# Dealing the columns of gathered expert rows over the U and V blocks: 42, 26, 35 and 33 instead of 45, 26, 35 and 30

## The chip, the cores and the metric

The kernel runs on one core of a Trainium2 chip. The metric is the device time of one execution in microseconds, as the median of several executions; less is better. "The profiled execution" is one more execution, recorded by the hardware profiler.

## The reference

One inference step of a hybrid decoder: a trunk layer (a Conformer convolution module and a Mamba-2 mixer that share their projections) and behind it a PEER expert mixer, which takes more than half of the time and which alone the change touches. It reads, cut to what matters:

```python
def peer_block(xb, w_q, keys, U, V):
    T = xb.shape[0]
    q = (xb @ w_q).reshape(T, PEER_HEADS, 2, D_KEY // 2)
    s = jnp.einsum('thcd,hckd->thck', q, keys).astype(jnp.float32)
    s1, i1 = lax.top_k(s[:, :, 0], PEER_TOPK)
    s2, i2 = lax.top_k(s[:, :, 1], PEER_TOPK)
...
```

From the 16 best keys of each half the 16 best pairs of each of 8 heads are chosen, so each token has 128 experts of 16,384, with softmax weights g. The result for a token x is the sum over its 128 experts e of g_e · gelu(U_e · x) · V_e, where U_e and V_e are rows of 1024 numbers. The mixer works on 320 tokens (256 of the prompt, 64 of the sample); its output, added to the trunk's and normalised, is `y`.

## The kernel before, in words

**Two ways to do the experts.** For 136 tokens the rows are gathered: 128 tokens with one token in each partition, and 8 extra tokens whose 128 experts are spread over 16 partitions each. A *column* is one expert of every partition: an indirect DMA (`gather`, L1152, issued on POOL) brings 128 rows of 2 × 1024 float32, U and V rows side by side, 1 MB, into one of five buffers `wuv`. VectorE (DVE) takes the dot product with the token (`pick_dot`, L1309), ScalarE (ACT) takes Gelu (L1311) and multiplies with the weight (L1314), and VectorE adds the weighted V row to `ygat` (`pick_sum`, L1319). There are 128 columns for the 128 tokens and 8 for the extra tokens, 136 in all, and one step behind them for the last sum.

For the other 184 tokens all experts are computed densely, in 128 blocks of 128 experts. `u_block` (L1416–1423) multiplies a block of U with the tokens in 8 matmuls on TensorE (PE) into PSUM, and ACT takes Gelu into S (L1423). `g_step` (L1429–1460) builds one-hot weights on VectorE, multiplies them on TensorE (L1449) into `pg`, and multiplies S by them. `v_block` (L1520–1523) multiplies S with a block of V into the accumulators `va`. All U blocks run first, then all V blocks.

**The blocks' weights.** Each block is one load of 512 KB into a ring of 8 slots (`bring`, `block`, L1386–1414); a load is issued when its slot comes free. From block 24 on, the odd blocks' loads are issued by ACT and the even ones' by SP (L1404). An engine issues in its own order: a load on ACT stands behind whatever ACT has to do before it, a column's Gelu among it, which itself waits for VectorE's dot.

**How columns stand among the blocks.** A gather waits for the block four steps earlier (`LEAD`), and gathers are issued four columns ahead of their use (two in the second half of V). The columns' steps, called `ops`, are dealt out in four parts by `NU` and `take`:

- during U blocks 0 to 83 together with the top-k work for the other tokens (`topk_tasks`) and the second half of the heads (`heads_tasks(HG)`, with the exp at L1133): NU[0] columns;
- during U blocks 84 to 127 with the steps of the first half of `g_step`: NU[1];
- during V blocks 0 to 63 with those of the second half: NU[2];
- during V blocks 64 to 126: what is left, the last sum among it.

`Feed` hands the tasks of a part out evenly: at each block it adds the part's summed costs, divided by its number of blocks, to a credit, and calls tasks while the credit lasts. Where a task is called sets its place and priority in the program; the order on each engine is then made by a scheduler from these.

The small transfers of the extra tokens' indices (`extra_columns`, L1293–1303) are called ahead of column 55's work, in the second part, but need only stand behind U block 70 (`XW`): the scheduler puts the four writes `xigd` on SP (L1298) among the loads of the blocks behind it, and later a read back (L1301).

**The end.** Behind block 126, `finish` (L1496–1518) normalises the 136 gathered tokens (squares on ACT, L1501, and products on DVE, L1517), and behind block 127 `finish_dense` (L1530–1544) does so for the 184 others (squares on ACT, L1535).

The lines that deal the columns:

```python
NU = (45, 26, 35)
LATER = 8
...
        bg = mixin(t1[:-1] + t2[:-5] + t1[-1:] + t2[-5:-1], take(NU[0] - 4 - LATER)) + take(4) + t2[-1:]
        bg += mixin(heads_tasks(HG), take(LATER))
...
        feed = Feed(bg, SB - 1)
...
        feed = Feed(mixin(g_tasks(0), take(NU[1])), 128 - SB - 2)
...
        feed = Feed(mixin(g_tasks(1), take(NU[2])), HB - 2)
...
        feed = Feed(take(len(ops)), LASTP - HB - 1)
```

Of the kernel before, what the change touches and what calls it, by code (L numbers as in the profile page):

```python
# [55 lines left out]
AGAIN = 24  # L56
HB = 64
KTILES = ((0, NGAT), (128, 128), (256, 64))
NU = (45, 26, 35)
LM = (0.05, 0.05, 0.1, 0.5, 0.999)  # L60
LOW = 400
NW0 = 3
# [96 lines left out]
def body(tc, ia, oa, stop=None):  # L159
    nc = tc.nc  # L160
    with ExitStack() as top:
# [1058 lines left out]
        def results(pool_, **kw):  # L1220
            lo, hi = parts[len(Sm)]
            p_ = top.enter_context(tc.tile_pool(name=pool_, bufs=1, **kw))
            Sm.append(p_.tile([128, hi - lo, ND], F32, name=f"S{len(Sm)}"))
            return p_
# [115 lines left out]
        def take(n):  # L1340
            t = ops[:n]
            del ops[:n]
            return t

        def mixin(a_, b_):
            out, na, nb = [], len(a_), len(b_)
            for q, t in enumerate(a_):
                out.append(t)
                out += b_[q * nb // na:(q + 1) * nb // na]
            return out  # L1350

        t1, t2 = topk_tasks(1), topk_tasks(2)
        bg = mixin(t1[:-1] + t2[:-5] + t1[-1:] + t2[-5:-1], take(NU[0] - 4 - LATER)) + take(4) + t2[-1:]
        bg += mixin(heads_tasks(HG), take(LATER))
# [108 lines left out]
        def g_tasks(half):  # L1463
            return [(2.8, lambda t=t: g_step(half, t)) for t in range(0, ND, GT)]
# [12 lines left out]
        s1p = results("s2p")  # L1477
        feed = Feed(mixin(g_tasks(0), take(NU[1])), 128 - SB - 2)
        for b in range(SB, 128):
# [65 lines left out]

        feed = Feed(mixin(g_tasks(1), take(NU[2])), HB - 2)
        for b in range(HB):
# [111 lines left out]
```

## Time and profile before

| | us |
|---|---|
| median of 3 runs | 1297.45 |
| lowest and highest | 1296.23, 1298.86 |
| the profiled execution | 1297.84 |
| its span, first to last instruction | 1296.1 |
| mean granted TensorE clock | 0.988 of full speed |

The U blocks run from about 542 to 945 us of the span and the V blocks from there to 1285. In the profile, PE is TensorE's matmuls, PEld its weight loads, DVE VectorE, ACT ScalarE, POOL GpSimd and SP SyncE; a q behind an engine's name is its issue of a DMA. `L1421` is a line of the program. `out<-in` are the names of the tiles: `eraw` a block's weights, `pj` and `va` accumulators in PSUM, `wuv` a gathered column, `scg` its dot products, `ygat` the gathered tokens' sum. "<-DMA eraw" in brackets behind an instruction means that it waited last for that load; the number ahead of it is how long the engine was idle. A row with "x16" stands for 16 records that follow each other: the 8 matmuls of a block have 16 records.

### The profile page before, as it was taken

How to read it: one execution, taken by the hardware profiler on the slowest of the kernel's cores; microseconds unless marked ns; L12 is line 12 of the kernel's file. 1: busy time of each engine (PE TensorE's matmuls, PEld its weight loads, DVE VectorE, ACT ScalarE, POOL GpSimd, SP SyncE). 2: the span in 40 equal slices, each digit the busy share in tenths (PEclk: the TensorE clock that was granted, in tenths of full speed). 3: DMA queues.
4: the chain of work that ended last, by engine and by line, in shares of the span. 5: the costliest groups of instructions: out<-in, count | busy, mean ns of one | idle time of the engine just before them, and what ended most of it. 6: DMA issues, size and time to landing. Idle time of an engine off the chain costs nothing.

```text
span 1296.1 us, 23646 instructions
## 1 busy us (share of the span) xinstructions
PE 1267.0 (98%) x8951; PEld 1220.6 (94%) x8951; DVE 953.3 (74%) x2095; ACT 531.7 (41%) x1339; POOL 599.2 (46%) x595
## 2 busy tenths in 40 slices
PE   9999999999999999999999898999999999999997
PEld 7989899898889999999999898999999999999997
DVE  6888778878877345549999968788888888545444
ACT  6888877788766444544222212122210110101102
POOL 2587777887785766974122222223332322122210
PEclk9999999999989999999999999999999999999999
DMA  6434444344433444766989999999999999999992
GB/s 247 175 130 175 178 172 175 138 167 174 139 121 137 153 156 147 254 225 233 375 332 416 415 415 416 410 413 414 415 414 416 414 415 414 399 413 414 412 411 94
DMA packets 85905, 373.77 MB, mean 288 GB/s; under 512 B 10000, under 2 KB 15376, under 8 KB 66208
## 3 DMA queue, kind: packets, MB, share of 16 engines
q1 hardware_dynamic: 48336, 166.82, 34.7%
q0 software_dynamic: 19584, 142.62, 27.0%
q10 hardware_dynamic: 17872, 62.84, 12.1%
q8 instruction: 70, 1.15, 0.4%
q14 instruction: 43, 0.35, 0.1%
HBM read 359.18 MB, written 13.06 MB: 287 GB/s over the span
## 4 chain that ended last, share of the span: by engine, by line
PE 64%; DVE 19%; DMA 9%; ACT 5%; issue 2%; POOL 1%; DVEq 0%; SPq 0%; POOLq 0%; ACTq 0%
PE va L1523 25%; PE pj L176 23%; PE pj L1421 11%; DMA wuv<-in_peer_uv_dram,gid 6%; DVE pcv L519 5%; DMA eraw<-in_uT_dram 3%; DVE pj L530 2%; DVE ygat L1319 2%; PE pg L1449 2%; DVE wuv L1309 1%; DVE st L712 1%; ACT L219 1%; ACT wh L243 1%; DVE dec L633 1%; PE pw L176 0%
## 5 line engine op out<-in xcount | busy, mean ns | idle before, releaser
L1152 POOL DMA_INDIRECT wuv<-in_peer_uv_dram,gid x136 | 173.9, 1278 | 483.5 <-PE va L1523 149.2
L247 POOL TENSOR_TENSOR wl<-wraw,wh 128x256 fp32r<-128x256 f32 (+1 forms) x202 | 288.6, 1449 | 105.5 <-ACT wh L243 57.0
L1523 PE MATMUL va<-S,eraw 128*128 128x184 f32 x2048 | 325.4, 320 | 0.0
L1523 PEld LDWEIGHTS va<-S,eraw 128*128 128x128 f32 x2048 | 318.9, 190 | 0.9 <-issue 0.9
L1421 PE MATMUL pj<-nd,eraw 128*128 128x184 f32 x1792 | 295.0, 324 | 9.8 <-DMA eraw<-in_uT_dram 9.7
L1421 PEld LDWEIGHTS pj<-nd,eraw 128*128 128x128 f32 x1792 | 282.8, 192 | 11.5 <-issue 11.0
L176 PE MATMUL pj<-ah,wh 128*128 128x336 f32 (+1 forms) x768 | 244.7, 329 | 0.5 <-ACT xnf L219 0.3
L1319 DVE SCALAR_TENSOR_TENSOR ygat<-wuv,scg,ygat 128x1024 f32<-128x1024 f32 x128 | 163.9, 1280 | 103.6 <-ACT scg L1314 103.5
L176 PE MATMUL pj<-al,wh 128*128 128x336 f32 (+1 forms) x768 | 234.5, 318 | 0.0
L1311 ACT ACTIVATE scg<-scg 128x1 f32<-128x1 f32 x136 | 27.3, 202 | 403.9 <-DVE wuv L1309 212.4
L1309 DVE SCALAR_TENSOR_TENSOR wuv<-wuv,x2m 128x1024 f32<-128x1024 f32 x128 | 155.9, 1218 | 19.1 <-DMA wuv<-in_peer_uv_dram,gid 19.0
L243 ACT CAST wh<-wraw 128x1024 fp32r<-128x1024 f32 x125 | 131.1, 1050 | 81.8 <-PE pj L176 62.3
L176 PEld LDWEIGHTS pj<-ah,wh 128*128 128x128 f32 x768 | 147.3, 192 | 4.3 <-ACT sz L219 0.8
L176 PEld LDWEIGHTS pj<-al,wh 128*128 128x128 f32 x768 | 146.9, 192 | 0.8 <-issue 0.2
L519 DVE SCALAR_TENSOR_TENSOR pcv<-ch,vec,pcv 128x320 f32<-128x320 f32 x232 | 127.8, 551 | 23.6 <-ACT pcv L517 21.1
L176 PE MATMUL pj<-ah,wl 128*128 128x336 f32 (+1 forms) x768 | 138.1, 315 | 0.0
L176 PEld LDWEIGHTS pj<-ah,wl 128*128 128x128 f32 x768 | 120.6, 189 | 0.3 <-DVE wl L342 0.2
L1423 ACT ACTIVATE S<-pj 128x184 f32<-128x184 f32 x128 | 38.7, 317 | 122.4 <-PE pj L1421 121.7
L530 DVE SCALAR_TENSOR_TENSOR pj<-mcat,vec,pj 128x360 f32<-128x360 f32 x96 | 56.7, 591 | 3.1 <-ACT pj L528 2.9
L1460 DVE SCALAR_TENSOR_TENSOR S<-pg,S 128x232 f32<-128x232 f32 (+1 forms) x92 | 34.7, 419 | 32.1 <-PE pg L1449 32.0
L219 ACT ACT_TABLE_LOAD x38 | 48.8, 1283 | 0.7
L1421 PE MATMUL pj<-nd,pre 128*128 128x184 f32 x256 | 42.0, 319 | 0.0
(388 smaller groups left out, 1691.8 us busy)
## 6 DMA issues: line engine op xcount, KB each, us to landing
wraw<-in_w_in_dram SPq DMA_DIRECT2D x80, 512.0 KB, 3.2
eraw<-in_vE_dram SPq DMA_DIRECT2D x64, 512.0 KB, 9.6
eraw<-in_vE_dram ACTq DMA_DIRECT2D x64, 512.0 KB, 9.6
eraw<-in_uT_dram SPq DMA_DIRECT2D x60, 512.0 KB, 9.1
eraw<-in_uT_dram ACTq DMA_DIRECT2D x52, 512.0 KB, 10.0
st<-in_state_dram SPq DMA_DIRECT2D x8, 1024.0 KB, 4.7
out_ssm_s_dram<-st SPq DMA_DIRECT2D x8, 1024.0 KB, 4.9
wraw<-in_w_mo_dram SPq DMA_DIRECT2D x16, 512.0 KB, 3.2
```

The lines of the kernel that those rows point to most:

```text
L176: i_ = nc.tensor.matmul(*a_, **kw)
L219: i_ = nc.scalar.activation(out, in_, f, **kw)
L243: (nc.vector.tensor_copy if on_dve else nc.scalar.copy)(h, src)
L247: (nc.gpsimd if on_pool else nc.vector).tensor_tensor(l[:, q:q + m], src[:, q:q + m], h[:, q:q + m].bitcast(F32), op=OP.subtract)
L519: nc.vector.scalar_tensor_tensor(to, in_, sc, eights(acc), op0=OP.mult, op1=OP.add)
L530: nc.vector.scalar_tensor_tensor(o, cat[:, w:w + n], wv, o, op0=OP.mult, op1=OP.add)
L1152: i_ = nc.gpsimd.indirect_dma_start(out=u, out_offset=None, in_=ia["peer_uv"], in_offset=bass.IndirectOffsetOnAxis(ap=gid[:, c:c + 1], axi ...
L1309: nc.vector.scalar_tensor_tensor(u[:, :D], u[:, :D], 1.0, x2m if c < NPICK else x2e, op0=OP.mult, op1=OP.mult, accum_out=w)
L1319: nc.vector.scalar_tensor_tensor(a_, u[:, D:], scg[:, c:c + 1], a_, op0=OP.mult, op1=OP.add)
L1421: i_ = nc.tensor.matmul(p[:, :ND], raw[:, k, :], nd[:, k, :], start=(k == 0), stop=(k == KD - 1))
L1423: nc.scalar.activation(Sv(b), p[:, :ND], AF.Gelu)
L1523: i_ = nc.tensor.matmul(va[k // 2][:, k % 2], raw[:, k, :], Sv(b), start=(b == 0 and k % 2 == 0), stop=(b == 127), skip_group_check=True)
```

## The change

One number of a table:

```diff
-NU = (45, 26, 35)
+NU = (42, 26, 35)
```

The first part is now given 42 columns instead of 45, the two middle parts 26 and 35 as before, and the last part what is left: 33 columns and the last sum instead of 30 and the last sum. The number of background tasks in the first part is as before, so the columns that are mixed among them stand further apart, and from about the twentieth on every column stands about three columns later against the blocks.

On ACT, around U block 53: the first rows are the Gelu and the scale of column 22 (`scg`), `pj` is a U block's Gelu, `gh` the exp of the second half of the heads, and `L1404` the load of block 53. Before:

```order
L1311 ACTIVATE scg<-scg 128x1
L1314 ACTIVATE scg<-scg,ggw 128x1
L1423 ACTIVATE S_7817<-pj 128x184
L1133 ACT_TABLE_LOAD
L1133 ACTIVATE gh<-gh,rsT 128x64
L1423 ACT_TABLE_LOAD
L1423 ACTIVATE S_7817<-pj 128x184
L1404 DMA eraw<-in_uT_dram 128x1024
```

Now, from the same column's Gelu; the first `L1404` is the load of block 53, the second that of block 55:

```order
L1311 ACTIVATE scg<-scg 128x1
L1314 ACTIVATE scg<-scg,ggw 128x1
L1423 ACTIVATE S_7811<-pj 128x184
L1404 DMA eraw<-in_uT_dram 128x1024
L1133 ACT_TABLE_LOAD
L1133 ACTIVATE gh<-gh,rsT 128x64
L1423 ACT_TABLE_LOAD
L1423 ACTIVATE S_7811<-pj 128x184
L1311 ACTIVATE scg<-scg 128x1
L1314 ACTIVATE scg<-scg,ggw 128x1
L1423 ACTIVATE S_7811<-pj 128x184
L1404 DMA eraw<-in_uT_dram 128x1024
```

Block 53's load has moved from behind the exp to ahead of it, and block 55's now stands behind the exp and one column's Gelu.

On ACT, from the load of block 63 to that of block 65. Before, three columns' Gelus stand between them:

```order
L1404 DMA eraw<-in_uT_dram 128x1024
L1423 ACTIVATE S_7817<-pj 128x184
L1311 ACTIVATE scg<-scg 128x1
L1314 ACTIVATE scg<-scg,ggw 128x1
L1311 ACTIVATE scg<-scg 128x1
L1314 ACTIVATE scg<-scg,ggw 128x1
L1311 ACTIVATE scg<-scg 128x1
L1314 ACTIVATE scg<-scg,ggw 128x1
L1423 ACTIVATE S_7817<-pj 128x184
L1404 DMA eraw<-in_uT_dram 128x1024
```

Now one column's Gelu stands between them:

```order
L1404 DMA eraw<-in_uT_dram 128x1024
L1311 ACTIVATE scg<-scg 128x1
L1314 ACTIVATE scg<-scg,ggw 128x1
L1423 ACTIVATE S_7811<-pj 128x184 x2
L1404 DMA eraw<-in_uT_dram 128x1024
```

At the end, behind ACT's last load of a V block, stand the Gelus of the last three columns where those of the last two stood. The order of SP's instructions around the writes `xigd` is as before.

## The prediction

> **What bounds the kernel now.** I read the page first (busy shares, DMA by slices), then the waits of TensorE, the windows by stage, and last the timelines around each wait and at the end.
>
> ```profile
> PE 1267.0 (98%) x8951; PEld 1220.6 (94%) x8951; DVE 953.3 (74%) x2095; ACT 531.7 (41%) x1339; POOL 599.2 (46%) x595
> DMA  6434444344433444766989999999999999999992
> PE pj L1421 <- DMA eraw<-in_uT_dram: 9.7, 5, 3.7
> ```
>
> TensorE is busy for 98% of the span, and from slice 21 (about 680 us) the DMA is full too. In the U and V blocks TensorE's waits for blocks' weights come to 9.7 us in 5 waits, the longest 3.7; all are for U. The windows (length, then busy time and count of PE, weight load, DVE, ACT, POOL; TensorE's clock; DMA share; GB/s) say where:
>
> ```profile
> 680.00:720.00 40.00, 38.78 (x248) 38.17 (x247) 38.61 (x106) 10.08 (x34) 11.10 (x9) 1.00 1.02 415
> 720.00:760.00 40.00, 36.56 (x230) 35.74 (x229) 35.44 (x87) 10.26 (x34) 10.37 (x9) 0.96 1.02 416
> 760.00:800.00 40.00, 38.52 (x296) 37.81 (x295) 28.43 (x48) 8.53 (x35) 10.21 (x8) 1.00 1.02 415
> 800.00:840.00 40.00, 36.29 (x277) 35.59 (x277) 30.06 (x55) 7.25 (x28) 11.67 (x7) 0.91 1.02 411
> 840.00:880.00 40.00, 40.00 (x330) 39.36 (x330) 33.53 (x63) 8.89 (x33) 12.64 (x9) 1.00 1.02 413
> 948.00:1108.00 160.00, 160.00 (x1306) 158.59 (x1305) 132.51 (x231) 17.73 (x71) 45.25 (x35) 1.00 1.02 415
> ```
>
> From 840 on TensorE is never idle, though the DMA moves the same 411 to 416 GB/s: what is lost is lost between 720 and 840. There it is three stalls, shown here with two undisturbed rows of the same matmul (start, us, then in brackets the idle time ahead and what ended it):
>
> ```profile
> 736.22 9.39 PE L1421 MATMUL pj<-nd,eraw 128*128 128x184 f32 x48 [3.33 <-DMA eraw<-in_uT_dram]
> 770.23 2.73 PE L1421 MATMUL pj<-nd,eraw 128*128 128x184 f32 x16 [1.48 <-DMA eraw<-in_uT_dram]
> 773.16 2.73 PE L1421 MATMUL pj<-nd,eraw 128*128 128x184 f32 x16
> 809.72 5.24 PE L1421 MATMUL pj<-nd,eraw 128*128 128x184 f32 x16 [3.71 <-DMA eraw<-in_uT_dram]
> 821.10 7.72 PE L1421 MATMUL pj<-nd,eraw 128*128 128x184 f32 x48
> ```
>
> They belong to blocks 53, 65 and 78. A stall costs more than its idle time when it is long: after 3.33 idle, 48 records took 9.39 instead of 7.72 (1.67 more), and after 3.71, 16 took 5.24 instead of 2.73 (2.51 more), where the granted clock falls to 0.96 and 0.91; after 1.48 nothing is added. So the three cost 5.00, 1.48 and 6.22, together 12.7 us.
>
> Why were the loads late? ScalarE (ACT) issues those of the odd blocks, in order with its other work:
>
> ```profile
> 720.77 0.20 ACT L1311 ACTIVATE scg<-scg 128x1 f32<-128x1 f32 x1 [5.56 <-DVE wuv L1309]
> 725.60 0.35 ACT L1133 ACTIVATE gh<-gh,rsT 128x64 f32<-128x64 f32 x1 [2.79 <-DVE gh L1131]
> 725.61 0.33 ACTq L1404 DMA_DIRECT2D eraw<-in_uT_dram  x1
> 727.71 0.33 ACTq L1404 DMA_DIRECT2D eraw<-in_uT_dram  x1
> 746.32 0.33 ACTq L1404 DMA_DIRECT2D eraw<-in_uT_dram  x1
> 760.26 0.20 ACT L1311 ACTIVATE scg<-scg 128x1 f32<-128x1 f32 x1 [4.50 <-DVE wuv L1309]
> 760.50 0.33 ACTq L1404 DMA_DIRECT2D eraw<-in_uT_dram  x1
> eraw<-in_uT_dram ACTq DMA_DIRECT2D x52, 512.0 KB, 10.0
> ```
>
> Block 53's load goes out at 725.61, right behind the exp that waited for VectorE; block 55's at 727.71. Block 65's goes out at 760.50, behind three columns' Gelus in a row, of which the last waited for VectorE until 760.26; the ACT load before it was at 746.32. A load of this queue lands 10.0 us after issue, so both come too late. Block 78's is SyncE's:
>
> ```profile
> SPq L1298 <- DMA eraw<-in_uT_dram: 7.5, 2, 4.4
> 782.01 8.73 SPq L1298 DMA_DIRECT2D xigd<-xig  x4
> 790.83 18.75 DMA eraw<-in_uT_dram
> ```
>
> Its load stands on SP behind the four small writes of the extra tokens' indices, which took from 782.01 for 8.73 us, and lands 18.75 us after 790.83.
>
> **What the change does, part by part.** No column's work is added or removed; each costs VectorE a dot and a sum (busy us and mean ns of one), 1.22 + 1.28 = 2.5 us:
>
> ```profile
> L1309 DVE SCALAR_TENSOR_TENSOR wuv<-wuv,x2m 128x1024 f32<-128x1024 f32 x128 | 155.9, 1218 | 19.1 <-DMA wuv<-in_peer_uv_dram,gid 19.0
> L1319 DVE SCALAR_TENSOR_TENSOR ygat<-wuv,scg,ygat 128x1024 f32<-128x1024 f32 x128 | 163.9, 1280 | 103.6 <-ACT scg L1314 103.5
> ```
>
> From about column 19 each stands some three columns later against blocks and background tasks, and three columns pass from U's first part to V's last. VectorE's 953.3 busy us and the bytes stay.
>
> *Block 53.* Its load now stands ahead of the exp, directly behind column 22's Gelu. That Gelu was at 720.77, and its dot stands behind some 2 us more of small VectorE work than before: load at 722.9. It took 736.22 − 725.61 = 10.6 us to be usable, so 733.5; TensorE was free at 736.22 − 3.33 = 732.9. Left is 0.6 of wait, too short to lower the clock, instead of 5.00: **−4.4**. If the dot is as late as the exp was, nothing is gained; if it isn't late, −5.0.
>
> *Block 55* takes 53's place behind the exp: load at an estimated 728.9 (727.71 and one Gelu more), usable at 738.9 by the 10.0. Its turn comes two blocks after 53's, 733.5 + 2 × 7.72/3 = 738.6, so 0.3 late, doubled for the unknown of the Gelu: **+0.7** (0 to 3, if the exp's wait of 2.79 grows).
>
> *Block 65.* One Gelu now stands between each two loads instead of three before one: up to two columns, 2 × 2.5 = 5 us, earlier, against 1.48 that it lacked. The 1.48 goes: **−1.5**.
>
> *Block 78.* SP's order is as before and the four writes still wait for loads that ACT issues (7.5 us). ACT's loads of those blocks move with TensorE's own progress, so I let the stall move along unchanged: **0**. The bounds: it takes back what was won (+5.2, if the writes' data set the time, not TensorE), or goes (−6.2).
>
> *Rest of U, V to block 63.* No wait is there (840 to 880: 40.00 of 40.00; 948 to 1108: 160.00 of 160.00) and the count of columns is as before: nothing but a shift earlier. What would end this cover is a load over 10 us late.
>
> *V from block 64.* Thirty columns instead of 27 are gathered between the same blocks. The queues' packets from 1150 to 1200 (packets, MB, share), the first and last of those gathers, a gather's landing, and the end:
>
> ```profile
> q0 software_dynamic: 1419, 10.31, 50.1%
> q10 hardware_dynamic: 1429, 5.21, 25.8%
> q1 hardware_dynamic: 1408, 5.13, 25.6%
> 1119.10 1.37 POOL L1152 DMA_INDIRECT wuv<-in_peer_uv_dram,gid  x1 [12.92 <-PE va L1523]
> 1253.26 1.13 POOL L1152 DMA_INDIRECT wuv<-in_peer_uv_dram,gid  x1 [3.85 <-PE va L1523]
> DMA to landing us min/median/max: 9.9/10.5/11.1
> 1267.32 1.22 DVE L1309 SCALAR_TENSOR_TENSOR wuv<-wuv,x2m 128x1024 f32<-128x1024 f32 x1
> 1270.52 0.63 ACT L1501 ACTIVATE wraw<-ygat 128x512 f32<-128x512 f32 x1 [1.41 <-DVE ygat L1319]
> 1272.66 0.63 ACT L1501 ACTIVATE wraw<-x2e 128x512 f32<-128x512 f32 x1 [1.41 <-PE va L1523]
> 1283.25 0.32 ACT L1535 ACTIVATE sqd<-va 128x184 f32<-128x184 f32 x1 [6.61 <-PE va L1523]
> ```
>
> The three queues have had the same number of packets, 1419, 1429 and 1408; the gathers' are twice as large. The Trainium skill, "DMA: Bandwidth & Descriptors", section "Queues, rings and completion order", says that each DMA engine goes round the queues that have work, packet by packet, and the trace agrees in these counts. By that rule three gathers more while the gather queue is never empty take nothing from the blocks' loads, and three fewer in U give them nothing. So the sum counts the order of ACT's loads alone; were the bytes shared instead, 3 × 1.049 MB at 415 GB/s would bring U's blocks up to 7.6 us sooner and V's as much later.
>
> The gather queue gets 10.31 MB per 50 us, one column of 1.049 MB per 5.09 us. Thirty then take 153 us: the last lands at 1119.10 + 152.7 = 1271.8 where it landed at 1253.26 + 9.9 = 1263.2, so 8.6 later against TensorE. Its dot began at 1267.32, 4.1 after that landing, so it comes 4.5 later. Behind it are 1.41 of ACT's wait at 1272.66 for TensorE and 6.61 idle ahead of the dense finish at 1283.25, of which about 4.2 lies beyond the last gathered step. 4.5 against 1.41 + 4.2 = 5.6: covered, by a margin of 1. I take **+1** for it (0 to 6.4; the upper end is the mean pace of before, 134.2 us from first issue to last and 9.9 to land, 144.1/27 = 5.34 a column: the thirtieth lands at 1279.3, 16.1 later, less 4.1 and 5.6).
>
> **The sum.** −4.4 + 0.7 − 1.5 + 0 + 1 = −4.2. The profiled execution took 1297.84 us (span 1296.1), so 1293.6; the median of the runs is 0.4 below it: **1293.2**. About 0.2%, 2.6 us, is what a measurement of this kernel tells from no change: faster is below 1294.85, slower above 1300.05.
>
> **Rivals.**
>
> *The waits only move (0.28).* DMA is full at 415 GB/s from 680 on, so blocks that are used sooner meet weights that are not sooner there. The five us come back at block 78, whose 18.75 of landing is the queues' backlog: −4.2 + 5.2 = +1.0, less 0.4 for the median: **1298.4**. For it: DMA share 1.02 in every window. Against it: SyncE's loads are issued far ahead, and 840 to 1108 has the same share and no wait.
>
> *More is won (0.13).* With fewer columns ahead of them, ACT's loads before the four writes go out sooner, the writes wait less and block 78's stall shrinks. All of it gone gives −4.2 − 6.2 = −10.4, 1287. Since the DMA is full, no load can gain without another's loss, so I price half, −3.1: 1297.84 − 4.2 − 3.1 − 0.4 = **1290**. For it: the writes' 7.5 us of waiting is for loads of this very queue. Against it: three columns' bytes less in that stretch do not reach the block queues by the equal packet counts above.
>
> *Slower, at the end (0.15).* One row more gives V's pace:
>
> ```profile
> 1120.00:1210.00 90.00, 90.00 (x580) 90.00 (x579) 41.64 (x51) 8.18 (x33) 20.47 (x19) 1.00 1.01 410
> ```
>
> A block's 16 records take 16 × 90/580 = 2.48 us. Now 34 steps (33 columns and the last sum) are spread over 62 blocks, one per 62 × 2.48/34 = 4.53 us, and the queue delivers one in 5.09: over thirty columns 30 × 0.56 = 17 us behind. The rival says that the finish of the gathered tokens then runs into the dense finish, which needs the same ACT and VectorE, so that only the dot's 4.1 and the 1.41 are slack: 17 − 5.5 = 11.5 on the end, less U's 5.2: +6.3, 1304 less 0.4, **1303.5**. It decides from a last column that is 4.1 + 1.41 + 5.2 = 10.7 later than before against TensorE; my sum has 8.6. For it: the DMA share of 1.01 in this row, so that the queue can't catch up. Against it: gathers are issued ahead of their turn and five buffers hold them, and before the change 31 steps came one per 62 × 2.48/31 = 4.96, faster than the queue's 5.09 too, and left 4.1 of slack at the dot.
>
> *The change doesn't do what it says:* excluded, the order of instructions shows the moves.
>
> **Range and chances.** The forecast has 0.44; its own terms reach from 1291 (block 53's −5.0, nothing at block 55 and the end) to 1295 (block 55's +2 more). Faster is the forecast and the larger gain, 0.57; the same is the moved waits, 0.28; slower 0.15. The range runs from 1288.5, near the larger gain's lower end, to 1299.0, the moved waits with the end's margin used up; it leaves out the 1303.5 and the last of the larger gain.
>
> **What would show it.** Right: block 53's load at about 723, ahead of the exp, its idle time under 1 and the clock of that window back at 1.00; no stall at block 65; block 78's stall of the same size, 5 us earlier; 840 to 1108 as full as before; the last dot some 4 us later against TensorE, and the idle time ahead of the dense finish shorter by about that. Wrong: a longer stall at block 78 (the waits moved), none there (more is won), or the dense finish released by the gathered finish instead of TensorE (the end).

## The result

| | before | after |
|---|---|---|
| median, us | 1297.24 (6 runs) | 1291.21 (6 runs) |
| lowest and highest | 1296.23, 1298.86 | 1288.42, 1293.13 |
| the profiled execution, its span | 1297.84, 1296.1 | 1292.40, 1290.6 |

The ratio of after to before is 0.9949, with a 95% interval of 0.9935 to 0.9963: 6.0 us faster by the medians, 5.4 between the two profiled executions. A second set of 11 runs of the changed kernel gave 1293.01 beside 1298.18 for the kernel before: 0.9966 (0.9953 to 0.9980). The forecast was 1293.2.

The page of the changed kernel:

```profile
PE 1262.9 (98%) x8951; PEld 1217.0 (94%) x8951; DVE 955.1 (74%) x2095; ACT 530.0 (41%) x1339; POOL 602.5 (47%) x595
DMA  6435444444433444765989999999999999999994
```

And TensorE's waits for loads:

```profile
PE pj L1421 <- DMA eraw<-in_uT_dram: 5.5, 2, 4.4
PE va L1523 <- DMA eraw<-in_vE_dram: 1.4, 1, 1.4
```

The waits for U's blocks have fallen from 9.7 us in 5 to 5.5 in 2; one of 1.4 us for a V block is new. The windows of U (length; busy time and count of PE, weight load, DVE, ACT, POOL; clock; DMA share; GB/s):

```profile
680.00:720.00 40.00, 40.00 (x258) 39.74 (x258) 39.34 (x116) 9.51 (x32) 9.88 (x9) 1.00 1.02 415
720.00:760.00 40.00, 38.88 (x257) 38.35 (x256) 31.73 (x73) 10.57 (x36) 9.97 (x8) 1.00 1.02 414
760.00:800.00 40.00, 38.49 (x305) 37.32 (x303) 29.05 (x48) 7.46 (x34) 9.54 (x8) 1.00 1.02 415
800.00:840.00 40.00, 36.91 (x284) 36.60 (x285) 33.09 (x60) 7.85 (x31) 9.15 (x8) 0.91 1.02 410
```

From 720 to 760 TensorE is idle for 1.1 us instead of 3.4 and its clock is back at 1.00; from 760 to 800 it is idle for 1.5 as before, but now 1.3 of that is the start of block 78's wait, where block 65's stood; from 800 to 840 it is much as before. The DMA is as full as it was. TensorE's two stalls in U:

```profile
736.66 2.73 PE L1421 MATMUL pj<-nd,eraw 128*128 128x184 f32 x16 [1.12 <-DMA eraw<-in_uT_dram]
803.09 4.93 PE L1421 MATMUL pj<-nd,eraw 128*128 128x184 f32 x16 [4.39 <-DMA eraw<-in_uT_dram]
```

ACT around block 53's load:

```profile
720.65 0.20 ACT L1311 ACTIVATE scg<-scg 128x1 f32<-128x1 f32 x1 [5.98 <-DVE wuv L1309]
720.89 0.33 ACTq L1404 DMA_DIRECT2D eraw<-in_uT_dram  x1
723.86 0.35 ACT L1133 ACTIVATE gh<-gh,rsT 128x64 f32<-128x64 f32 x1 [1.17 <-DVE gh L1131]
726.71 0.33 ACTq L1404 DMA_DIRECT2D eraw<-in_uT_dram  x1
```

Block 53's load goes out at 720.89, ahead of the exp at 723.86, and block 53 does not wait. Block 55's, behind exp and one Gelu, goes out at 726.71 and is 1.12 us late. Block 65 does not wait. Block 78 waits as before, 4.39 us.

The end: ACT's first square of the dense finish,

```profile
1277.82 0.32 ACT L1535 ACTIVATE sqd<-va 128x184 f32<-128x184 f32 x1 [2.59 <-DVE wraw L1517]
```

VectorE's last dot of a column and last products of the gathered finish,

```profile
1267.59 1.23 DVE L1309 SCALAR_TENSOR_TENSOR wuv<-wuv,x2m 128x1024 f32<-128x1024 f32 x1 [3.46 <-DMA wuv<-in_peer_uv_dram,gid]
1275.18 2.43 DVE L1517 SCALAR_TENSOR_TENSOR wraw<-x2e,frs,wuv 128x512 f32<-128x512 f32 x2
```

and TensorE's last four V blocks:

```profile
1269.17 10.24 PE L1523 MATMUL va<-S,eraw 128*128 128x184 f32 x64 [1.36 <-DMA eraw<-in_vE_dram]
```

Before, the dense finish waited 6.61 us and TensorE released it; now it waits 2.59 and VectorE's gathered finish releases it. The last dot, which before came 4.9 us behind the last packet of its column, now waits for the landing (3.46).

**Where the time went.** By the start of each block's first matmul in TensorE's two timelines, TensorE is ahead of its former time by 0.4 us at block 0; by 2.2 at block 51; by 7.6 at block 54 (block 53's stall is gone); by 6.3 at block 55 (its new wait); by 8.2 at block 66 (block 65's stall is gone); by 7.3 from block 89 through V; and by 5.7 at the last V block, since V block 124 waited. The dense finish starts 1.06 us behind the start of the last V block, before 0.82. That leaves 5.4 to 5.5 at the end.

### The profile page after: what moved, and what is told of

Same layout as the page of the kernel before. It is cut to its first block, busy times and chain, and to the rows that moved or that the text cites. A ratio compares the mean times of both kernels' runs of the same rounds, so it can differ in the third digit from the quotient of the medians.

```text
span 1290.6 us, 23645 instructions
## 1 busy us (share of the span) xinstructions
PE 1262.9 (98%) x8951; PEld 1217.0 (94%) x8951; DVE 955.1 (74%) x2095; ACT 530.0 (41%) x1339; POOL 602.5 (47%) x595
## 3 DMA queue, kind: packets, MB, share of 16 engines
q10 hardware_dynamic: 17872, 62.84, 12.2%
## 4 chain that ended last, share of the span: by engine, by line
PE 60%; DVE 20%; DMA 10%; ACT 6%; issue 3%; POOL 1%; POOLq 0%; ACTq 0%; DVEq 0%; SPq 0%
PE va L1523 23%; PE pj L176 22%; PE pj L1421 11%; DMA wuv<-in_peer_uv_dram,gid 5%; DVE pcv L519 5%; DMA eraw<-in_uT_dram 3%; DVE pj L530 2%; PE pg L1449 2%; DVE wuv L1309 1%; DVE ygat L1319 1%; ACT L219 1%; DMA wuv<-in_fnorm_dram 1%; DVE st L712 1%; ACT wh L243 1%; POOL wl L247 1%
## 5 line engine op out<-in xcount | busy, mean ns | idle before, releaser
L1152 POOL DMA_INDIRECT wuv<-in_peer_uv_dram,gid x136 | 176.7, 1299 | 474.6 <-PE va L1523 107.6
L1314 ACT ACTIVATE scg<-scg,ggw 128x1 f32<-128x1 f32 x136 | 39.7, 294 | 6.9 <-PE va L1523 2.8
```

Of the source, the lines that this page charges most:

```text
L1152: i_ = nc.gpsimd.indirect_dma_start(out=u, out_offset=None, in_=ia["peer_uv"], in_offset=bass.IndirectOffsetOnAxis(ap=gid[:, c:c + 1], axi ...
L1314: nc.scalar.activation(w, w, AF.Copy, scale=ggw[:, c:c + 1])
```

## The experiments

The theory on record was that ACT's loads are late where they stand behind an operation that waits for VectorE, so that the gain is the gain of an order. After the first profile two rivals stood against it. *Bytes*: the DMA is full, and three columns' bytes, 7.6 us of it, have left U's first part. *VectorE*: three columns' work, 7.5 us, has left it too. In the expectations of the third and fourth run, the theories A and B are about what then sets the end: A has the DMA, which is full whatever the deal, and B TensorE or the last columns. From the fifth run on, B is the bytes' rival and D that of VectorE's work. In what follows "52 to 55" is the time from the start of block 52 to that of block 55, and so on; three undisturbed blocks take 7.5, and up to 8.1 where the one-hot matmuls stand between. Behind each time stands its ratio to the kernel before, timed beside it, with the 95% interval; the experiments ran in three sets, each on its own chip, so the ratios compare better across sets than the times do.

**The loads of blocks 53, 55 and 65 by SP**

```diff
-(nc.scalar if i % 2 and (name == "vE" or i > LATE) else nc.sync)
+(nc.scalar if i % 2 and (name == "vE" or i > LATE and i not in (53, 55, 65)) else nc.sync)
```

> The columns are dealt as before the change (45, 26, 35, 30); only the loads of U blocks 53, 55 and 65 are issued by SP instead of ACT. Theory (the order of ACT's loads behind Gelus and the exp makes the stalls): the stalls at blocks 53 (5.0 us) and 65 (1.5) go, TensorE enters V 6 to 7 us earlier, and the time falls by 5 to 6.5 us, to 1291 to 1292.5, with no column moved. Rival (three columns' bytes less in U's first part let the loads land sooner): no column is moved, so the loads land no sooner, stalls of the same sum, 1297 within 1 us.

Measured: 1297.81 us, 1.0008 (1.0000 to 1.0017). TensorE's stalls between blocks 51 and 80:

```profile
729.59 12.73 PE L1421 MATMUL pj<-nd,eraw 128*128 128x184 f32 x80 [0.64 <-ACT S L1423]
748.22 10.29 PE L1421 MATMUL pj<-nd,eraw 128*128 128x184 f32 x64 [2.72 <-ACT scg L1311]
759.39 12.71 PE L1421 MATMUL pj<-nd,eraw 128*128 128x184 f32 x80 [0.88 <-DMA eraw<-in_uT_dram]
812.44 4.33 PE L1421 MATMUL pj<-nd,eraw 128*128 128x184 f32 x16 [7.05 <-DMA eraw<-in_uT_dram]
```

The stalls at 53 and 65 are gone, as the theory said: with no column and no byte moved, 52 to 55 takes 7.5 instead of 12.7 and 64 to 67 takes 8.0 instead of 9.7. So it was the loads' place on ACT that made these two. But the gain is not there. At block 57 TensorE now waits 2.72 for ACT, which stood at a column's Gelu with the U blocks' own Gelus behind it (that Gelu had waited 1.86 for VectorE's dot); block 78, whose load is on the SP queue that now has three loads more, waits 7.05 instead of 3.71. U from block 32 to 128 takes 273.0 against 270.4 before; 2.5 more is lost ahead of block 50, where two profiles of one kernel, the change, differ by 1.6 as well. Taking the loads off ACT moves waits, it does not end them. The theory's number fails here, and the rival of the prediction that waits only move holds for this edit.

**The last part alone**

```diff
-NU = (45, 26, 35)
+NU = (45, 26, 32)
```

> Dealt 45, 26, 32, 33: U is as before the change, and the last part has three columns more. Theory (the three columns more are covered at the end): U's three stalls stay, 0 to +1 us, 1297 to 1298. Rival of the prediction (the gather queue falls 17 us behind and the gathered finish runs into the dense one): the end comes 6 to 11 us later, 1303 or more.

Measured: 1297.31, 1.0004 (0.9993 to 1.0014). TensorE in U:

```profile
736.77 7.76 PE L1421 MATMUL pj<-nd,eraw 128*128 128x184 f32 x48 [2.62 <-DMA eraw<-in_uT_dram]
771.56 4.35 PE L1421 MATMUL pj<-nd,eraw 128*128 128x184 f32 x16 [3.58 <-DMA eraw<-in_uT_dram]
812.80 4.41 PE L1421 MATMUL pj<-nd,eraw 128*128 128x184 f32 x16 [3.79 <-DMA eraw<-in_uT_dram]
```

ACT's first square of the dense finish:

```profile
1285.76 0.32 ACT L1535 ACTIVATE sqd<-va 128x184 f32<-128x184 f32 x1 [3.30 <-PE va L1523]
```

U's three stalls are at the same blocks as before the change. TensorE still releases the dense finish, with 3.30 of idle time ahead instead of 6.61. That is not all slack: where VectorE releases it, 2.6 stand there too, so about 0.7 is left. With TensorE as late as it was, three columns more at the end cost nothing that the timing can tell; the rival of 1303 is out.

**Three columns to V's first part instead of the last**

```diff
-NU = (42, 26, 35)
+NU = (42, 26, 38)
```

> Dealt 42, 26, 38, 30: U as after the change, the last part as before it. TensorE was 7.3 us earlier through U and V after the change but the end only 5.5. Theory A (the DMA, full from 680 us on, ends at the same time whatever the deal, and what waits for it last gives the 1.8 back): same as after the change within 1 us, 1290 to 1292. Theory B (the 33 columns of the last part give it back): the 1.8 comes too, 1289.4.

Measured: 1294.64, 0.9987 (0.9975 to 0.9999), so no faster than the change, and slower by its first set, though not clear of its second (0.9953 to 0.9980): B's time is out, and A's is missed by 2.6 us. Its one profile has a span of 1292.0. U is as after the change at blocks 53, 65 and 78, but takes 265.5 from block 32 to 128, against 263.5 and 264.7. The last column's dot comes at 1266.70 instead of 1267.59, and TensorE releases the dense finish, as B has it; from the start of V's second half to the end that is worth 1.1 and 0.2 us against the two profiles of the change. Why its median is slower by more than its profile shows stays open.

**The four writes apart**

```diff
-                          ustep[XW])
+                          ustep[XW - 9 + up * 6 // 64 + 3 * c_])
```

> As after the change, but the four small writes on SP stand behind blocks 61, 64, 67 and 70 instead of all behind block 70, so that none holds SP for long. Both theories: the stall at block 78 (4.4 us idle and 2.2 of slow clock, 6.6) goes and TensorE is over 6 us earlier in V. Theory A (the DMA's end sets the end): the gain is given back by waits for V's loads or the last columns, 0 to 2 us faster, 1289 to 1291. Theory B (TensorE sets the end): 5 to 6.6 faster, 1284.6 to 1286.2.

Measured: 1292.33, 0.9966 (0.9952 to 0.9980): no faster than the change. SP's first of the four writes:

```profile
754.69 0.34 SPq L1298 DMA_DIRECT2D xigd<-xig  x1
```

TensorE's stall:

```profile
796.67 4.41 PE L1421 MATMUL pj<-nd,eraw 128*128 128x184 f32 x16 [2.25 <-DMA eraw<-in_uT_dram]
```

And the start of the dense finish on ACT:

```profile
1278.19 0.32 ACT L1535 ACTIVATE sqd<-va 128x184 f32<-128x184 f32 x1 [2.58 <-DVE wraw L1517]
```

No write holds SP for more than 0.4 us now, and 77 to 80 takes 9.5 instead of 15.0. But a stall of 2.25 has come up at block 76, U as a whole takes 263.1 against 263.5 and 264.7 in the two profiles of the change, and the dense finish is released by VectorE as after the change. So "over 6 us earlier in V" failed, which both theories had, B's time is out by 6 us, and A's is missed by 1.3; since the premise failed, the run does not decide between them.

**Half the bytes of six columns in U**, dealt as before the change

```diff
-NU = (45, 26, 35)
+NU = (45, 26, 35); HALF = (20, 23, 26, 29, 32, 35)
-            i_ = nc.gpsimd.indirect_dma_start(out=u, out_offset=None, in_=ia["peer_uv"],
+            v = ia["peer_uv"].rearrange("e (h d) -> (e h) d", h=2) if c in HALF else ia["peer_uv"]; i_ = nc.gpsimd.indirect_dma_start(out=u[:, :D] if c in HALF else u, out_offset=None, in_=v,
-            nc.vector.scalar_tensor_tensor(a_, u[:, D:], scg[:, c:c + 1], a_, op0=OP.mult, op1=OP.add)
+            nc.vector.scalar_tensor_tensor(a_, u[:, :D] if c in HALF else u[:, D:], scg[:, c:c + 1], a_, op0=OP.mult, op1=OP.add)
```

> Dealt as before the change (45, 26, 35, 30); six columns of U's first part (20, 23, 26, 29, 32, 35) gather rows of half the length, so 3.1 MB, three columns' worth, are left out, and VectorE adds the half that is there: its work is the same. From U block 32 to block 90 TensorE took 167.5 us before the change, 168.0 and 170.1 in two other runs with 45 columns, 160.7 after it. Theory B (U's first part is bound by the bytes that the full DMA must move): 161 within 2, and 6 to 7 us less in all, 1290 to 1291. Theory D (VectorE's work in the columns, 2.5 us each, makes ACT's loads late): 167 to 170, and 1296.6 within 1. The theory of the prediction (only where the loads stand on ACT) goes with D here unless the order happens to mend.

**Half of VectorE's work for the same columns**

```diff
-NU = (45, 26, 35)
+NU = (45, 26, 35); HALF = (20, 23, 26, 29, 32, 35)
-            nc.vector.scalar_tensor_tensor(u[:, :D], u[:, :D], 1.0, x2m if c < NPICK else x2e,
+            m = D // 2 if c in HALF else D; nc.vector.scalar_tensor_tensor(u[:, :m], u[:, :m], 1.0, (x2m if c < NPICK else x2e)[:, :m],
-            nc.vector.scalar_tensor_tensor(a_, u[:, D:], scg[:, c:c + 1], a_, op0=OP.mult, op1=OP.add)
+            m = D // 2 if c in HALF else D; nc.vector.scalar_tensor_tensor(a_[:, :m], u[:, D:D + m], scg[:, c:c + 1], a_[:, :m], op0=OP.mult, op1=OP.add)
```

> The counterpart of the run with half the bytes: dealt as before the change, all bytes gathered, but for the same six columns VectorE takes the dot and the sum over half the width only, 7.5 us of VectorE less, as three columns would be. Theory B (bytes): block 32 to 90 stays at 167 to 170, 1296.6 within 1. Theory D (VectorE's work): 161 within 2, 1290 to 1291.5.

Measured: with half the bytes 1291.69, 0.9954 (0.9940 to 0.9968); with half of VectorE's work 1297.51, 0.9999 (0.9990 to 1.0008). Both kernels leave out part of the six columns' work, so only their times count, not their output. Block 32 to 90 took 163.6 and 168.7. That looks like a verdict for the bytes, though with half the bytes the 163.6 lies between the two theories' bands; but the order of instructions had moved in both. ACT with half the bytes, load of block 53 and exp:

```profile
725.74 0.33 ACTq L1404 DMA_DIRECT2D eraw<-in_uT_dram  x1
729.78 0.35 ACT L1133 ACTIVATE gh<-gh,rsT 128x64 f32<-128x64 f32 x1 [2.03 <-DVE gh L1131]
```

TensorE there, at blocks 53 and 78:

```profile
735.88 7.87 PE L1421 MATMUL pj<-nd,eraw 128*128 128x184 f32 x48 [1.50 <-ACT scg L1311]
806.00 5.24 PE L1421 MATMUL pj<-nd,eraw 128*128 128x184 f32 x16 [3.66 <-DMA eraw<-in_uT_dram]
```

ACT with half of VectorE's work:

```profile
727.29 0.35 ACT L1133 ACTIVATE gh<-gh,rsT 128x64 f32<-128x64 f32 x1 [1.72 <-DVE gh L1131]
728.34 0.33 ACTq L1404 DMA_DIRECT2D eraw<-in_uT_dram  x1
```

and TensorE there, at block 53:

```profile
738.78 10.08 PE L1421 MATMUL pj<-nd,eraw 128*128 128x184 f32 x48 [4.20 <-DMA eraw<-in_uT_dram]
```

With half the bytes the load of block 53 stands ahead of the exp, as after the change. What became shorter there is 52 to 55 (12.7 to 9.3) and 64 to 67 (9.7 to 8.0), where the order moved; the stall at block 78, where it didn't, is the same. With half of VectorE's work the load still stands behind the exp, and the stall is longer, 4.20. So this pair speaks against VectorE's work as the sole cause, and does not separate bytes from order. The next four do that better.

**The count swept: 39, 48, 41 and 43 columns in the first part**

```diff
-NU = (42, 26, 35)
+NU = (39, 26, 35)
```

and in the same way 48, 41 and 43.

> Dealt 39, 26, 35, 36: three columns more taken out of U's first part. Theory B: block 32 to 90 falls by about 6.8 again, to 154 (not under 152.7, which is the 160.7 less the 8 of stalls left after the change). But the DMA's last bytes still come at about 1270 and the last gathered column with them, and the end was 23 us behind that column's landing after the change: no more gain, 1291 to 1296. If TensorE's time in U sets the end: 1284 to 1285.

> Dealt 48, 26, 35, 27: three columns more in U's first part. Theory B: block 32 to 90 rises by three columns' bytes, 3 x 1.049 MB at 415 GB/s = 7.6 us, to 175 within 2, and the end follows TensorE: 1303 within 2. The theory of the prediction (where the loads happen to stand on ACT): no rule in the count, 1292 to 1300.

> Dealt 41, 26, 35, 34. Theory B: TensorE is 2.2 to 2.5 us earlier than after the change at the end of U, but the last column's dot is later (1267.6 with 42, 1269.7 with 39, so about 1268.3) and the end with it: 1291.5 to 1294. If TensorE set the end: 1289.

> Dealt 43, 26, 35, 32. Theory B: one column's bytes more in U, TensorE 2.2 to 2.5 us later than after the change and the end with it: 1293.5 within 1. The theory of the prediction (which load happens to stand behind which Gelu): no rule, 1289 to 1297.

**The changed kernel again**, without an edit

> The changed kernel once more, beside its neighbours on one chip: 1291.2 within 1.5, and a second profile of the stalls in U. Theory B: they may lie at other blocks than in the first profile, but block 32 to block 128 takes 263.5 within 2.5 us, as with 42 columns in the three profiles so far (263.1 to 265.5).

Measured: 39 gives 1296.73, 1.0000 (0.9987 to 1.0012); 48 gives 1304.39, 1.0052 (1.0035 to 1.0070); 41 gives 1296.37, 0.9992 (0.9982 to 1.0001); 43 gives 1295.71, 0.9987 (0.9974 to 1.0000); the changed kernel again 1293.01, 0.9966 (0.9953 to 0.9980), a little over its expected band. The bands that theory B gave for 39, 41 and 43 were missed by 0.7, 2.4 and 1.2 us; the time with 48 lies inside B's band and 4.4 us above that of the prediction's theory. ACT with 43, the exp and the load of block 53:

```profile
726.49 0.35 ACT L1133 ACTIVATE gh<-gh,rsT 128x64 f32<-128x64 f32 x1 [2.79 <-DVE ci L1062]
726.50 0.33 ACTq L1404 DMA_DIRECT2D eraw<-in_uT_dram  x1
```

and TensorE with 43, at block 53:

```profile
736.55 9.40 PE L1421 MATMUL pj<-nd,eraw 128*128 128x184 f32 x48 [2.77 <-DMA eraw<-in_uT_dram]
```

One column more than the change, and the load is back behind the exp and the stall is back at block 53, while block 65 has none. All the profiles together but that of the loads by SP, where block 53's load is not on ACT (from the starts of the blocks and of ACT's instructions, us; the last run with 42 is described below):

| columns in the first part, kernel | load 53 and the exp | 52 to 55 | Gelus ahead of load 65 | 64 to 67 | 77 to 80 | U, 32 to 128 |
|---|---|---|---|---|---|---|
| 48 | behind | 10.4 | 3 | 13.4 | 10.9 | 277.3 |
| 45, before | behind | 12.7 | 3 | 9.7 | 14.8 | 270.4 |
| 45, last part alone | behind | 10.3 | 3 | 13.5 | 13.8 | 270.9 |
| 45, half of VectorE's work | behind | 14.3 | 1 | 8.0 | 14.3 | 271.5 |
| 45, half the bytes | ahead | 9.3 | 2 | 8.0 | 14.7 | 266.5 |
| 43 | behind | 12.2 | 1 | 8.0 | 15.8 | 269.6 |
| 42, after | ahead | 8.8 | 1 | 8.0 | 15.0 | 263.5 |
| 42, after, again | ahead | 9.9 | 1 | 8.0 | 13.9 | 264.7 |
| 42, more in V | ahead | 8.8 | 1 | 8.0 | 15.2 | 265.5 |
| 42, writes apart | ahead | 8.5 | 1 | 8.0 | 9.5 | 263.1 |
| 42, half the bytes at the end | ahead | 9.6 | 1 | 8.0 | 14.2 | 265.4 |
| 41 | ahead | 7.6 | 1 | 7.7 | 15.4 | 263.6 |
| 39 | ahead | 7.5 | 1 | 8.0 | 8.1 | 257.5 |

Wherever block 53's load stands behind the exp, 52 to 55 takes 10.3 to 14.3, and wherever ahead, 7.5 to 9.9; wherever three Gelus stand ahead of block 65's load, 64 to 67 takes 9.7 or more, elsewhere 8.0 or less. The time of U falls in steps, when a load changes its place (43 to 42: 269.6 to 263.5), and hardly moves from 42 to 41, which also takes a column's bytes out. A price per column's bytes would give 2.5 us at each step. Block 32 to 90, on which the bytes' rival was staked, takes 168.3, 167.5, 166.8, 160.7, 160.8 and 154.7 with 48, 45, 43, 42, 41 and 39 columns: the rival's 154 for 39 was met, its 175 for 48 was missed by nearly 7.

That 48 is slower all the same comes from one place that neither theory had. Of the 6.9 us that its U takes longer than before the change, 6.5 lie between blocks 98 and 101, where TensorE waited for VectorE's one-hot weights, not for a load:

```profile
873.33 1.29 PE L1449 MATMUL pg<-oh 128*128 128x64 f16 x16 [3.03 <-DVE oh L1445]
```

Over the whole sweep, 48 to 39, U falls by 19.8, 2.2 per column, so columns and stalls do go together on the long run; that bytes have no part in it is not shown. In these profiles the load stands ahead of the exp exactly where no more than 42 columns' bytes are gathered in the first part, so bytes and order change together there; it is the run with the loads by SP that parts them for blocks 53 and 65.

The other end of the sweep shows the second limit. The first square of the dense finish with 41:

```profile
1282.88 0.32 ACT L1535 ACTIVATE sqd<-va 128x184 f32<-128x184 f32 x1 [2.58 <-DVE wraw L1517]
```

With 39:

```profile
1279.90 0.32 ACT L1535 ACTIVATE sqd<-va 128x184 f32<-128x184 f32 x1 [2.57 <-DVE wraw L1517]
```

And TensorE's waits for V's loads with 39:

```profile
PE va L1523 <- DMA eraw<-in_vE_dram: 3.2, 2, 3.0
```

Of the 5.1 us by which the span is longer with 41 than after the change (1295.7), 2.1 lies ahead of U: block 0 starts at 544.1 instead of 542.0 (over all fourteen profiles it starts between 540.7 and 544.1, though no edit touches what stands ahead of it). The rest is the end: the dense finish starts 3.5 us behind the start of the last block instead of 1.1, since the last column's dot comes at 1272.65. With 39, TensorE is through U 6.0 us sooner than after the change, and all of it and more is lost in the last part: V's blocks 64 to 127 take 167.5 us from first start to last start instead of 163.2, and the gathered finish then holds the dense one for 5.8 us behind the start of the last block.

**Half the bytes of six columns in the last part**, of the changed kernel: the edit of the run with half the bytes in U, with `HALF = (100, 104, 108, 112, 116, 120)`

> As after the change, but six columns of the last part (100, 104, 108, 112, 116, 120) gather rows of half the length, 3.1 MB or three columns' worth less, with VectorE's work the same. In the eight profiles so far the span ended 13.6 to 13.7 us after the last V block began or 23.0 us after the last column's dot began, whichever was later; after the change both give the same (1276.76 + 13.7 and 1267.59 + 23.0). Theory B (bytes): the last column's dot comes some 5 us earlier, TensorE's wait of 1.4 for V's block 124 goes, and TensorE alone sets the end, 1.5 to 2 us earlier than after the change: 1289 to 1290. If something else in the last part set the end: as after the change, 1291.2 within 1.

Measured: 1291.35, 0.9958 (0.9947 to 0.9970), which the timing can't tell from the change's 0.9966 beside it. Its profile:

```profile
1276.50 0.32 ACT L1535 ACTIVATE sqd<-va 128x184 f32<-128x184 f32 x1 [5.27 <-PE va L1523]
```

TensorE releases the dense finish again, with 5.27 of idle time ahead, the wait for V block 124 is gone, and V's second half takes 161.6 instead of 163.2 and 162.1. The mechanism is as theory B has it; from the start of V's second half to the end of the span it is worth 1.8 and 0.9 us against the two profiles of the change. B's time of 1289 to 1290 is missed by 1.4, so this rests on the profile alone.

## Why the prediction was right, and where it was not

**Block 53** (forecast −4.4). From the start of block 52 to that of block 54 TensorE took 5.2 us less, in the second profile of the change 4.7. The load was expected at 722.9 and left at 720.89; TensorE was 2.3 ahead by then, so against TensorE it left as forecast, within 0.3. It was usable within 9.5 us instead of 10.6, so the 0.6 of remaining wait was not there; in the second profile 0.31 of it was. Two runs show the cause: with the loads by SP the stalls at 53 and 65 are gone though all columns and bytes are as before, and at 43 the stall comes back with the load behind the exp. Why the change keeps this gain, where the loads by SP lost it again at blocks 57 and 78, the order of these loads does not explain, and what part the bytes and VectorE's work have in that stays open.

**Block 55** (+0.7): +1.3, the wait of 1.12 that took 53's place; +1.8 in the second profile.

**Block 65** (−1.5): 64 to 67 became 1.7 shorter in both profiles.

**Block 78** (0): 77 to 80 went from 14.8 to 15.0, and to 13.9 in the second profile. Right, and neither bound was touched. That the stall's cause is SP's writes is shown in part: apart, they end most of it, and part of it comes back earlier; and with 39 columns the four writes, behind one another as before, hold SP for 2.07 us only, where they hold it for 4.9 to 8.7 in the other twelve profiles, and block 78 does not wait.

**The rest of U.** The sum had nothing for the two short waits of before at blocks 37 and 39, 1.2 us of the 9.7. In the first profile of the change they are gone and 34 to 50 is 1.5 shorter; in the second, 34 to 50 takes 42.1 as before. So this 1.5 is not the change's, and U's gain is −5.7 by the second profile, against a sum of −5.2.

**The end** (+1): between +0.9 (second profile) and +1.8. The size is near, the step failed in its working. The prediction had the last column land 8.6 us later against TensorE, its dot 4.5 later, and 5.6 of slack: covered. It landed 4.4 us later on the clock, 1266.81 against 1262.38 (packets in the trace), with TensorE 7.3 earlier: 11.7 later. The dot came 0.3 later on the clock, 7.6 against TensorE. Less the 5.6 that is 2.0 not covered, about the 1.8 found. V block 124's wait, which the prediction put at nothing, cost nearly as much at the same time: it took TensorE's lead from 7.3 to 5.7. Each alone would have brought the end to within 0.3 of where it came. What was missed is how late the last column lands in a full queue: it was issued at 1245.96 and landed 20.9 us later, where the sum had used 9.9 from issue to landing for the last one and 5.09 per column for the pace.

The sum: −4.2 forecast, −5.4 between the profiled executions, −4.7 with the second profile's 1293.11 us in place of the first. That it came so near is in part luck: in the first profile U gave more than its terms (7.3 of lead against 5.2) and the end took more than its own (1.8 against 1). And one of the prediction's signs of being wrong did show: the dense finish is released by the gathered finish instead of TensorE.

**The rivals.** That the waits only move was wrong for this change and right for the two edits that moved loads or writes by hand. That more is won: its time, 1290, is nearer to the first median than the forecast, but its mechanism did not come, since block 78's stall stayed; the stall went at 39 columns, and there the end took the gain. The slower end was wrong at 42 columns in size: the last column came 11.7 later against TensorE, past the 10.7 from which that rival decides, but cost about 2 and not 11.5 (by its own terms that rival comes to 1303.7, not 1303.5). It is the limit that ends the sweep: at 41 and 39 the gathered finish sets the end.

**The packets' rule of the prediction.** By it three columns fewer don't bring U's blocks sooner, and three more cost V's nothing. For U the run with half the bytes is no test of it, since six columns there have as many packets as before, each half as large; on bytes it says that where the order was as before (block 78; 34 to 50 at 43.7 against 42.0), no wait became shorter. For V the rule fell short. With 30 columns in the last part no profile has a wait for a V load. With 33, the change's two profiles have 1.4 and 0.2 us of it and the one with the writes apart 1.9; with 34 it is 1.8, with 36 3.2. With 33 of which six are half as long it is gone, and also with 33 behind a U as late as before. So more columns behind a TensorE that is ahead did make V's loads late.

## What to carry to other kernels

When loads are issued by an engine that also computes, look up for each late load what stands just ahead of it on that engine and what that waits for; a table of counts moves such loads by one place at a time, so its effect here came in steps, and one value was no guide to the next. Before pulling work out of a stretch that stalls, find both limits of the end, here the last block and the last gathered column: the gain lasts until the second meets the first. A wait that is ended by handing the load to another queue may come up again on that queue.

## What the runs showed of the hardware

The end has a simple form that the prediction didn't use: in all fourteen profiles the span ended 13.6 to 13.7 us after the start of the last V block, or 23.0 after the last column's dot, whichever was later. Before it was 1282.43 + 13.7 = 1296.1; with 39 columns, 1269.69 + 23.0 = 1292.7. After the change both give it, 1276.76 + 13.7 = 1290.5 and 1267.59 + 23.0 = 1290.6: 42 is where the two limits meet.

What a stall costs beyond its idle time is not told by the idle time alone. With 43 columns, after 2.77 us idle, 48 records took 9.40 instead of 7.72, and from 737 to 740 the granted clock was 0.50; with the last part alone, after 2.62 idle at the same block, they took 7.76, and the clock there was 1.00. With the writes apart 2.25 idle were enough for 16 records to take 4.41 instead of 2.73, at a clock of 0.50 from 797.5 to 800.5. The prediction's rule that a stall costs more "when it is long" is thus not enough. So some 1.7 us of the spread of 52 to 55 in the table is this clock and not a load that was later.
